# 58 expert blocks instead of 56 get their first product before the expert loop, and 0.62 and 2.0 gathers per block instead of 0.60 and 1.98

## The chip, the cores and the metric

The kernel runs on one core of a Trainium2 chip. The metric is the device time of one execution in microseconds. The core has a matrix engine (PE, with PEld for its weight loads), a vector engine (DVE), an activation engine (ACT), GpSimd (POOL), and SyncE (SP), which here only issues DMAs. Each engine works through its instructions in order. DMAs are issued on the queues of SP, POOL and ACT.

## The reference

Two groups of tokens (128 of a prompt, 512 of a latent grid, D = 1024) go through two layers that share their weights. Layer 0 mixes with a short gated convolution, layer 1 with a bidirectional Mamba-2 scan; each is followed by the channel mixer that this change touches, PEER:

```
q = (t @ wq).reshape(T, 8 heads, 2, 128);  s = einsum(q, keys)       # two lists of 128 scores
s1, i1 = top_k(s[:, :, 0], 16);  s2, i2 = top_k(s[:, :, 1], 16)
cand = s1[..., :, None] + s2[..., None, :]                            # 256 candidates
sc, pos = top_k(cand, 16);  idx = take(i1 * 128 + i2, pos);  g = softmax(sc)
act = einsum('td,thkd->thk', t, u[idx])                               # 16384 experts, rows of u and v
out = einsum('thk,thkd->td', gelu(act) * g, v[idx])
```

So every token picks 8 x 16 experts of 16384, and each expert is one row of `u` and one of `v`.

## The kernel before

**Two ways through the experts.** For 464 of the 512 latent tokens (ND) the kernel computes all experts densely. The 16384 experts are 128 blocks of 128. The first product of block a ("U block", `u_blocks`, L502) is a 128 x 464 matrix of u-rows times tokens: 8 slices of K, and `mm3` (L126) does each in three matmuls of split operands (hi*hi, hi*lo, lo*hi), so 24 matmuls of 464 columns. ACT takes the Gelu (L511) into a tile `ga` of the pool `ring`, which has LAG + 2 = 5 buffers. The second product ("V block", in the loop at L651) multiplies `ga` with the dense gate matrix of the block and accumulates v-rows: 24 matmuls as well, 18 into six PSUM banks `acc` and two times three into a rotating bank `rot`, which DVE adds into `sacc` (L647, L649). Gates are zero where a token did not pick an expert.

For the other 48 latent tokens and the 128 prompt tokens the kernel gathers the picked rows instead: NG = 16 + 32 + 128 = 176 gathers, each an indirect DMA on POOL's queue (L592) of 128 rows of u and v (1 MB) into one of three buffers `uv`; DVE makes the dot with the token rows `hrow` (L599) and adds gate times v-row to `cacc` (L609). The three groups of columns begin at gathers 0, 16 and 48 (G0). At 16 and 48 the token rows change: `next_rows` loads a new `hrow` over the old one, which has one buffer, and `last_tokens` folds `cacc` with small matmuls on PE (L622, L623).

**Order of the stages in one PEER layer.** Gates first (`peer_gates`, L751): queries, scores and top-k on DVE, then 29 chunks of one-hot products that write the dense gate matrix to `gdram` in device memory. Beside that DVE-heavy work PE has time, and `fill(ns)` (L521) lets it do U blocks in portions, eight steps to a block, each step counted as 650 ns; NSP caps how many blocks. A block below NSP has its `ga` stored to `adram` in device memory by POOL's queue (L513) and loaded again by SP's queue before its V block (`load_act`, L567).

Then the handover, in this order of the program (from L627): `gather(0)`, `gather(1)` and the first gate tile `gt` on POOL's queue, all U blocks up to NSP - 1 that are not done yet, `load_act` of blocks 0 to 2, `make_h(0)` and `make_h(1)` (gate times activation on DVE at L577, its rounding on ACT at L581, the rest on DVE at L586), and the last U block:

```
fill(0, NSP * KT - state["n"] - KT)
for a in range(LAG):
    load_act(a)
make_h(0); make_h(1)
fill(1e9)
```

**The loop** runs over a = 0 to 125. While a + LAG < NSP an iteration holds one V block and one `load_act`; after that one V block and U block a + LAG (L658). From the last chunks of the gates on the order of the instructions is that of the program (`manual_schedule`). Gathers are placed by a credit: each iteration adds GATHER[0] (no U block) or GATHER[1] (with one), and for each whole unit one gather, one dot and one addition are issued; an iteration ends its gathers early at a group's start. Loads of U, V and gate tiles run on SP's queue through `Stream` (L72): two raw buffers, ACT makes the high part (L92), DVE the low part (L101), and the load of the next block waits until the split two blocks before is done.

Of the kernel before, what the change touches and what calls it, by code (L numbers as in the profile page):

```python
# [31 lines left out]
HALF = 320  # L32
EPS = 1e-6
NBLK = 128
NSP = 56
LAG = 3
GA = 4
TB = 16
# [1 line left out]
SW = 64  # L40
CH = 5
FILL_Q = (0, 8500)
GATHER = (0.60, 1.98)
START = 4
MORE = (1, 1, 0, 4)
ADA_C = 16
# [70 lines left out]
class K:  # L117
# [28 lines left out]
    def run(s):  # L146
        nc, A = s.nc, s.A
        with ExitStack() as ctx:
# [4 lines left out]
            s.gdram = dram.tile([NBLK // GA, P, ND // SG, GA, SG], F32, name="gdram")  # L153
            s.adram = dram.tile([NSP, P, ND], F32, name="adram")
            s.sdram = dram.tile([1, 2, D], F32, name="sdram")
# [328 lines left out]
    def peer(s, i):  # L484
        nc, A = s.nc, s.A
        with ExitStack() as ctx:
# [15 lines left out]
            def u_blocks():  # L502
                for a in range(NBLK):
# [7 lines left out]
                    nc.scalar.activation(g, pa, AF.Gelu)  # L511
                    if a < NSP:
                        nc.gpsimd.dma_start(s.adram[a], g)  # L513
# [7 lines left out]
            def fill(ns, steps=0):  # L521

                state["owe"] += ns
                while (steps > 0 or ns and state["owe"] > 0) and state["n"] < NSP * KT:
                    t = next(ub)
                    if not steps:
                        state["owe"] -= t
                    steps -= 1 if steps else 0
                    state["n"] += 1
                U.split(state["n"] // KT + 2)  # L530
# [8 lines left out]
            with ExitStack() as mc:  # L539
# [27 lines left out]
                def load_act(a):  # L567
                    if a < NSP:
                        t = ring.tile([P, ND], F32, name="ga")
                        nc.sync.dma_start(t, s.adram[a])  # L570
                        ga[a] = t
# [60 lines left out]
                state["owe"] = 0  # L632
                fill(0, NSP * KT - state["n"] - KT)
                for a in range(LAG):
# [16 lines left out]
                for a in range(NBLK - 2):  # L651
                    V.high(a + 2)
                    if a + LAG >= NSP:
                        U.high(a + LAG + 2)
# [21 lines left out]

                    credit += GATHER[0] if a + LAG < NSP else GATHER[1]
                    due, before = 0, slot
# [793 lines left out]
```

## Time and profile before

| what | value |
|---|---|
| time, median of 3 runs | 4063.26 us (4061.71 to 4071.17) |
| profiled execution, its own time | 4057.71 us |
| its span, first to last instruction | 4056.0 us |
| granted PE clock, mean | 0.987 |
| busy: PE, DVE, ACT, POOL | 97%, 84%, 41%, 13% |
| DMA: moved, mean rate | 979.15 MB, 241 GB/s |

The two expert loops lie at about 787 to 1815 us and 2999 to 4027 us of the span. The profile's times are from the start of the span. An idle time is shown in square brackets behind an instruction, with what ended it. A busy PE is a pipeline of matmuls, each of which shows a duration longer than the distance to the next one.

### The profile page before, as it was taken

To read this page: it belongs to the slowest core of one execution; us is meant where nothing else is said; L and a number is where in the kernel's file an instruction comes from. 1 tells how busy PE (TensorE), PEld (TensorE's weight loads), DVE (VectorE), ACT (ScalarE), POOL (GpSimd) and SP (SyncE) were. 2 spreads that over 40 slices of the span, in tenths; PEclk is the share of its full clock that TensorE was granted. 3 is DMA by queue.
4 is the path that set the end of the run, shared out by engine and by line. 5 is a ranking of instruction groups with operands and counts; after the bars stand their busy time and mean duration, and the time that the engine had idled before them with its cause. 6 is when DMAs were issued, how large, how long until landed. Compare 5 with 4: busy or idle time off the path is not lost.

```text
span 4056.0 us, 59421 instructions
## 1 busy us (share of the span) xinstructions
PE 3915.4 (97%) x22237; PEld 3548.9 (87%) x22237; DVE 3394.0 (84%) x6512; ACT 1663.2 (41%) x3120; POOL 514.9 (13%) x695
## 2 busy tenths in 40 slices
PE   8999999899999999999999999999989999999998
PEld 6989988788888888888899998998878888888887
DVE  8978988588878888887999856998768888888887
ACT  5233344433334333336555644334433333343333
POOL 0010000011112212211110101000011111121211
PEclk9999999999999999999999999999999999999999
DMA  6643258988889989973333234226888898998995
GB/s 228 218 154 121 83 171 248 287 318 312 329 311 338 341 325 333 339 274 126 114 102 119 88 114 173 83 99 192 251 296 314 316 334 316 337 335 329 333 333 222
DMA packets 337451, 979.15 MB, mean 241 GB/s; under 512 B 39371, under 2 KB 174795, under 8 KB 291081
## 3 DMA queue, kind: packets, MB, share of 16 engines
q1 hardware_dynamic: 146922, 508.73, 35.7%
q0 software_dynamic: 64000, 398.47, 26.4%
q10 hardware_dynamic: 126240, 68.16, 5.9%
q8 instruction: 174, 2.85, 0.3%
q14 instruction: 115, 0.94, 0.1%
HBM read 867.00 MB, written 108.14 MB: 240 GB/s over the span
## 4 chain that ended last, share of the span: by engine, by line
issue 41%; PE 29%; DVE 15%; POOL 9%; DMA 4%; ACT 2%; POOLq 0%; SPq 0%; ACTq 0%; DVEq 0%
POOL uv L592 9%; PE pact L128 2%; DMA ur<-uT 2%; PE pact L130 2%; PE pj L128 2%; PE pact L129 2%; PE pj L129 2%; PE pj L130 2%; DVE ul L101 2%; DVE wl L101 1%; PE bank L128 1%; PE bank L129 1%; PE bank L130 1%; PE bank L1189 1%; PE pg L999 1%
## 5 line engine op out<-in xcount | busy, mean ns | idle before, releaser
L128 PE MATMUL pact<-hnh,uh 128*128 128x464 f32 x2048 | 774.2, 378 | 1.0 <-DVE xt L623 1.0
L130 PE MATMUL pact<-hnh,ul 128*128 128x464 f32 x2048 | 768.3, 375 | 0.0
L129 PE MATMUL pact<-hnl,uh 128*128 128x464 f32 x2048 | 766.6, 374 | 0.0
L592 POOL DMA_INDIRECT uv<-uv,cidx x352 | 362.2, 1029 | 1698.6 <-DVE cacc L609 1567.2
L128 PE MATMUL acc<-h,wh 128*128 128x464 f32 x1536 | 575.4, 375 | 0.0
L130 PE MATMUL acc<-h,wl 128*128 128x464 f32 x1536 | 575.3, 375 | 0.0
L129 PE MATMUL acc<-h,wh 128*128 128x464 f32 x1536 | 573.1, 373 | 0.0
L92 ACT ACTIVATE wh<-wr 128x1024 fp32r<-128x1024 f32 x385 | 404.9, 1052 | 377.8 <-DMA wr<-uv 92.5
L599 DVE SCALAR_TENSOR_TENSOR uv<-uv,hrow 128x1024 f32<-128x1024 f32 x352 | 430.1, 1222 | 128.5 <-DMA uv<-uv,cidx 125.3
L101 DVE TENSOR_TENSOR wl<-wr,wh 128x1024 fp32r<-128x1024 f32 x385 | 469.8, 1220 | 54.7 <-ACT wh L92 54.4
L609 DVE SCALAR_TENSOR_TENSOR cacc<-uv,dg,cacc 128x1024 f32<-128x1024 f32 x346 | 443.4, 1282 | 0.0
L130 PEld LDWEIGHTS pact<-hnh,ul 128*128 128x128 f32 x2048 | 386.4, 189 | 45.5 <-DVE ul L101 0.3
L128 PEld LDWEIGHTS pact<-hnh,uh 128*128 128x128 f32 x2048 | 387.2, 189 | 44.6 <-DVE xt L623 1.3
L129 PEld LDWEIGHTS pact<-hnl,uh 128*128 128x128 f32 x2048 | 387.2, 189 | 44.3
L511 ACT ACTIVATE ga<-pact 128x464 f32<-128x464 f32 x256 | 141.8, 554 | 582.6 <-PE pact L130 578.9
L101 DVE TENSOR_TENSOR ul<-ur,uh 128x1024 fp32r<-128x1024 f32 x256 | 312.1, 1220 | 56.0 <-ACT uh L92 55.9
L92 ACT ACTIVATE uh<-ur 128x1024 fp32r<-128x1024 f32 x256 | 268.3, 1050 | 184.7 <-PE pact L129 81.0
L129 PEld LDWEIGHTS acc<-h,wh 128*128 128x128 f32 x1536 | 291.0, 189 | 36.0
L130 PEld LDWEIGHTS acc<-h,wl 128*128 128x128 f32 x1536 | 290.0, 189 | 34.9
L128 PEld LDWEIGHTS acc<-h,wh 128*128 128x128 f32 x1536 | 290.7, 189 | 33.8
L601 ACT ACTIVATE dg<-dg 128x1 f32<-128x1 f32 x352 | 70.6, 200 | 540.4 <-DVE uv L599 540.0
L586 DVE TENSOR_TENSOR h<-h,h 128x464 fp32r<-128x464 f32 x256 | 163.8, 640 | 127.7 <-PE rot L129 123.8
(346 smaller groups left out, 7978.1 us busy)
## 6 DMA issues: line engine op xcount, KB each, us to landing
ur<-uT SPq DMA_DIRECT2D x256, 512.0 KB
wr<-uv SPq DMA_DIRECT2D x256, 512.0 KB
gt<-gdram SPq DMA_DIRECT2D x62, 928.0 KB
gdram<-st ACTq DMA_DIRECT2D x28, 2048.0 KB
mw<-ada_wT SPq DMA_DIRECT2D x80, 512.0 KB
adram<-ga POOLq DMA_DIRECT2D x112, 232.0 KB, 4.1
ga<-adram SPq DMA_DIRECT2D x112, 232.0 KB
wr<-ssd_w SPq DMA_DIRECT2D x48, 512.0 KB
```

The lines of the kernel that those rows point to most:

```text
L92: s.K.nc.scalar.activation(hi.rearrange("p a b -> p (a b)"), s.raw[s.nh], AF.Copy)
L101: s.K.nc.vector.tensor_sub(lo.rearrange("p a b -> p (a b)"), s.raw.pop(s.ns), hi.rearrange("p a b -> p (a b)").bitcast(F32))
L128: mm(out, wh, mh, start=start, stop=False)
L129: mm(out, wh, ml, start=False, stop=False)
L130: mm(out, wl, mh, start=False, stop=stop)
L511: nc.scalar.activation(g, pa, AF.Gelu)
L586: nc.vector.tensor_sub(h2, h, h1.bitcast(F32))
L592: nc.gpsimd.indirect_dma_start(out=t[:], out_offset=None, in_=A["uv"].rearrange("l e d -> (l e) d"), in_offset=bass.IndirectOffsetOnAxis(a ...
L599: nc.vector.scalar_tensor_tensor(UV[n][:, :D], UV[n][:, :D], 1.0, rows[-1], op0=ALU.mult, op1=ALU.mult, accum_out=dg[:, n:n + 1])
L601: nc.scalar.activation(dg[:, n:n + 1], dg[:, n:n + 1], AF.Gelu)
L609: nc.vector.scalar_tensor_tensor(cacc, t[:, D:], dg[:, n:n + 1], cacc, op0=ALU.mult, op1=ALU.add)
L999: nc.tensor.matmul(g[:, q, :], oh[:, t + q, :], o1[:, t + q, :], start=True, stop=False)
```

## The change

Two constants at the head of the file. NSP goes from 56 to 58: in each layer 58 blocks have their U product, their store to `adram` and their load from it ahead of the loop or in its first part, and `adram` has 58 slots. The loop has 55 iterations without a U block instead of 53, and 71 with one instead of 73 (two more at the end carry V alone in both). GATHER goes from (0.60, 1.98) to (0.62, 2.0).

```diff
-NSP = 56
+NSP = 58
 LAG = 3
@@
 FILL_Q = (0, 8500)
-GATHER = (0.60, 1.98)
+GATHER = (0.62, 2.0)
```

The places that read them: the cap of `fill` (L524), the store or keep decision (L512), `load_act` (L568), the handover (L633) and the loop (L653, L658, L677, L682).

## Rows read from the trace of the kernel before

**Rows 1.** The page, part 1: busy time, share of the span, instructions.

```profile
PE 3915.4 (97%) x22237; PEld 3548.9 (87%) x22237; DVE 3394.0 (84%) x6512; ACT 1663.2 (41%) x3120; POOL 514.9 (13%) x695
```

**Rows 2.** Waits of PE, whole span: who waited for whom, us, times, longest.

```profile
PE rot L128 <- ACT ga L511: 18.2, 2, 9.7
PE rot L128 <- DVE sacc L649: 15.8, 11, 3.9
...
PE rot L128 <- DVE sacc L647: 6.2, 2, 3.6
```

**Rows 3.** Timeline of PE, layer 0: start, us, engine, line, operation [idle before].

```profile
763.05 0.46 PE L128 MATMUL pact<-hnh,uh 128*128 128x464 f32 x1
...
778.05 0.38 PE L130 MATMUL pact<-hnh,ul 128*128 128x464 f32 x1
786.91 0.75 PE L128 MATMUL rot<-h,wh 128*128 128x464 f32 x1 [8.48 <-ACT ga L511]
...
796.54 0.67 PE L128 MATMUL rot<-h,wh 128*128 128x464 f32 x1 [3.61 <-DVE sacc L647]
```

**Rows 4.** Timeline of PE, the handover of layer 1.

```profile
2999.50 0.76 PE L128 MATMUL rot<-h,wh 128*128 128x464 f32 x1 [9.71 <-ACT ga L511]
```

**Rows 5.** Stretches: length, busy (count) of PE, PEld, DVE, ACT, POOL, PEclk, DMA share, GB/s.

```profile
849.00:899.00 50.00, 50.00 (x240) 44.68 (x239) 41.90 (x58) 18.34 (x33) 6.57 (x6) 1.00 0.90 326
1230.00:1330.00 100.00, 100.00 (x478) 89.26 (x477) 87.33 (x110) 39.10 (x80) 20.30 (x20) 1.00 0.91 346
```

**Rows 6.** Timeline of POOL, which issues its DMAs, at the handover.

```profile
774.45 0.59 POOL L564 DMA_DIRECT2D gt<-gdram  x1
775.01 1.66 POOL L513 DMA_DIRECT2D adram<-ga  x3
```

**Rows 7.** DMA queues from 773 to 785: packets, MB, share.

```profile
q0 software_dynamic: 599, 3.69, 87.4%
```

**Rows 8.** DMA queues from 785 to 787.

```profile
q0 software_dynamic: 25, 0.07, 8.8%
```

**Rows 9.** Timeline of DVE at the handover.

```profile
784.59 1.19 DVE L577 TENSOR_TENSOR h<-ga,gt 128x464 f32<-128x464 f32 x2 [8.41 <-DMA gt<-gdram]
```

**Rows 10.** DMA queues from 793 to 799: q1 is SP's, q0 POOL's.

```profile
q1 hardware_dynamic: 511, 1.36, 58.6%
q0 software_dynamic: 159, 1.07, 42.2%
```

**Rows 11.** Timeline of SP, which issues its DMAs, at the handover.

```profile
785.26 0.32 SPq L570 DMA_DIRECT2D ga<-adram  x1
785.68 0.42 SPq L84 DMA_DIRECT2D ur<-uT  x1
```

**Rows 12.** Waits of SP's queue from 763 to 800.

```profile
SPq L570 <- DVE h L577: 11.3, 1, 11.3
```

**Rows 13.** Timeline of ACT at the handover.

```profile
789.70 1.06 ACT L92 ACTIVATE uh<-ur 128x1024 fp32r<-128x1024 f32 x1 [2.84 <-DMA ur<-uT]
```

**Rows 14.** DMA issues of the whole span: count, KB each, median us to landing.

```profile
TT<-cdram POOLq DMA_DIRECT2D x40, 8.0 KB, 2.6
```

**Rows 15.** Stretches around gathers 16 and 48 in both layers, columns as above.

```profile
924.00:950.00 26.00, 25.35 (x120) 22.04 (x119) 17.30 (x26) 8.35 (x15) 3.12 (x3) 0.93 0.82 291
1142.00:1230.00 88.00, 84.69 (x400) 74.65 (x399) 67.49 (x86) 30.88 (x64) 17.19 (x16) 0.98 0.84 307
3131.00:3163.00 32.00, 29.84 (x143) 26.34 (x142) 21.65 (x32) 9.83 (x17) 3.13 (x3) 0.95 0.74 270
3365.00:3480.00 115.00, 112.67 (x540) 99.79 (x540) 95.31 (x122) 42.68 (x87) 22.19 (x22) 1.00 0.90 332
```

**Rows 16.** Timeline of SP at the change of `hrow` for gather 48.

```profile
1144.21 0.33 SPq L615 DMA_DIRECT2D hrow<-hdram  x1
```

**Rows 17.** Timeline of DVE at the same change.

```profile
1150.58 1.23 DVE L599 SCALAR_TENSOR_TENSOR uv<-uv,hrow 128x1024 f32<-128x1024 f32 x1 [1.05 <-DMA hrow<-hdram]
```

**Rows 18.** Timeline of PE at the folds there.

```profile
1156.69 1.87 PE L622 MATMUL pact<-fold,cacc 128*128 128x32 f32 x16
```

## The prediction

> **What bounds the kernel now.** I read the page first: PE is busy for 97% of the span [rows 1], so a change pays only where PE stands idle or runs for nothing. Next the list of who waited for whom, for PE over the whole span [rows 2]: the longest entry is two waits, one per layer, 18.2 us together, of `rot` for the Gelu at L511; two waits for the first copy into `sacc` (L647) add 6.2 us, and eleven for the sums at L649 15.8 us. Then the timeline of PE at the first two [rows 3, 4]. The reader is to see a handover. The last one-hot products end at 763.05, three U blocks follow back to back until 778.05 plus 0.21, then PE stands for 8.48 us, does seven eighths of V block 0, and stands for another 3.61 us. Layer 1 repeats it with 9.71 and 2.6 us. Last the stretches [rows 5]: in the loops PE is busy for all of 50 and all of 100 us, 478 matmuls in 100 us or 0.209 us each, 24 of them or 5.02 us per block, with the DMA engines busy for 90 and 91%. So the loops are paced by PE with DMA close behind, and the handover is where PE has nothing to do.
>
> **What the change moves.** The fills beside the gates ask for about 416 steps of U work (8 by number, 265.6 us at 0.65 us), that is 52 blocks; 53 were done at 763.05. The old cap of 56 is not reached there, so nothing beside the gates changes. The two added blocks run in the handover, behind the three that run there today: 48 matmuls at 0.209 are 10.0 us of PE in each layer. The same 10.0 us leave the loop: two iterations fewer carry a U block. PE's total is unchanged, and the gain is as much of 10.0 us per layer as falls into time in which PE is idle.
>
> **What ends the gap, step by step (layer 0).** POOL's queue issues two gathers (1.05 MB each), the gate tile `gt` at 774.45 (0.95 MB) and from 775.01 the stores of the last three U results (0.24 MB each) [rows 6]; that makes 3.76 MB. POOL's queue moved 3.69 MB of it between 773 and 785 [rows 7] and the last 0.07 MB after [rows 8], so the burst ends at about 785.3. The product at L577 waits 8.41 us for `gt` until 784.59 [rows 9], and 2.32 us later (two products, two roundings, the Gelu of block 55 behind them on ACT) PE starts at 786.91 [rows 3].
>
> With 58, PE has blocks 53 to 56 and 57 to do: 778.3 + 10.0 = 788.3, if their U data is there. It is: the loads have a buffer as soon as the split two blocks before is done, so the two added ones go out by about 771 and 776, ahead of the three `adram` loads on SP's queue. Two costs come with them.
>
> First, the load at 776 moves 0.52 MB beside the burst. [rows 10] show a stretch where both queues have work, and both move: 1.36 and 1.07 MB in 6 us. At the burst's 0.31 MB per us the burst then ends 1.7 us later, at 787.0; the bounds are 0 (the load is served after it) and 3.4 (both added loads fall into it). The Trainium skill (DMA: Bandwidth & Descriptors, section Queues, rings and completion order) says that each DMA engine takes turns between the queues that have work, a packet at a time. By that rule the 1.7 us are due; if queues were served in order of issue, the term would be 0 and each layer would gain 1.7 us more.
>
> Second, the ring of activations has five buffers. Today `adram` loads 0 and 1 find two that are free long before, and only load 2 is late: it goes out at 785.26 [rows 11], having waited 11.3 us for the first product at L577 to end [rows 12]. With 58 the five buffers hold blocks 52 to 56, so loads 0, 1 and 2 all wait for stores that stand at the end of POOL's burst. Load 0 goes out at 787.0 instead of before 770, and the first product waits for it, no longer for `gt`. Its landing: a U load of 512 KB took 4.0 us (785.68 to 789.70 [rows 11, 13]) and an 8 KB load 2.6 us [rows 14]; for 232 KB I take 3.2, so 790.2, and with the same 2.32 us PE starts at 792.5. The idle time falls from 8.5 to 4.2 us.
>
> The second stall is set by ACT, which in order waits 2.84 us for the next U load until 789.70 [rows 13]; 6.84 us after that PE goes on at 796.54. That load now stands behind three loads instead of one: about 788.3 to issue, 4.0 to land, 0.3 for the data ahead of it, so 792.6, and PE goes on at 799.4. (PE by itself gets there at 792.5 + 6.02 = 798.5, the 6.02 being 796.54 - 3.61 - 786.91.) So PE goes on 2.9 us later than today with 10.0 us more behind it: **7.1 us per layer, 14 for both**; layer 1 runs the same chain against a gap of 9.7 us [rows 4]. Bounds: 20 us if all of the added work is covered, 9 if burst and landing take their upper values (795.0 and 801.8: 4.7 per layer).
>
> **The gathers.** From the code's own arithmetic, 31 gathers in the 53 U-free iterations become 34 in 55, and the rest go from 145 in 73 (with one iteration of three and two of one) to 142 in 71, all of two. DMA per U-free iteration: V 0.52, activation 0.24, gate 0.24, gathers 0.62 x 1.05 = 0.65, in all 1.65 MB in 5.02 us or 328 GB/s; with two gathers and a U load 3.38 MB in 10.04 us, 337. The trace carries 346 for 100 us with PE busy throughout [rows 5], so both fit, by a few per cent. The extra stores and loads of activations (two of each per layer, 0.95 MB) are in these sums.
>
> The change of `hrow` at gather 48 becomes dearer in one way and cheaper in another. Today it costs PE, counted as stretch less 0.209 per large matmul (all but the 16 folds): 88 - 384 x 0.209 = 7.7 us and 115 - 524 x 0.209 = 5.5 us [rows 15], part of it from the iteration of three gathers after it. With 58 gathers 46 and 47 fall into one iteration, so the load of the new rows, which took 6.4 us from issue to the dot that uses it (1144.21 to 1150.58 [rows 16, 17]), stands between them: dot 47 at 1149.5 (today's 1150.58 less its wait of 1.05), the load issued behind it at 1150.7 and landed at 1157.1, its dot and addition 47 behind it until about 1159.5 (2.4, the 1.22 of L599 and 1.28 of L609 overlapping), against folds that start at 1156.69 today [rows 18]: 2.8 us of PE. Add 1.9 for the folds [rows 18] and 1.8 for the lower granted clock (1.2 of 2.4 GHz) behind such a stop (0.07 of 26 us around gather 16 [rows 15]): 6.5, or 13.0 for both layers against 13.2. I take 0 (-8 to +6). The change at gather 16 costs 26 - 104 x 0.209 = 4.3 and 32 - 127 x 0.209 = 5.5 us today [rows 15]; it moves one iteration forward, away from the iteration that loads a gate tile: -1 (-4 to +3).
>
> **Sum.** -14 + 0 - 1 = -15 us against the profiled execution's 4057.7 (span 4056.0): 4042.7. That execution lies 5.6 us under the median of the three timed runs, 4063.3, so the median becomes **4048**.
>
> **Rivals.**
> 1. *The gap is covered altogether* (-20 and cheap `hrow` changes, -5: 4038). For it: 8.5 + 3.6 and 9.7 + 2.6 us of idle time exceed 10.0. Against it: the ring wait, which puts a load between the burst and the first product.
> 2. *The gap only moves* (about -6: 4057). Loads 0 to 2 and the U load after them wait behind a burst that the added stores and loads lengthen by more than I took; the lower bound above, 9, less what dearer `hrow` changes cost, some 3. For it: DMA is at 0.31 MB per us there and everything in the chain is a transfer.
> 3. *Slower*: the loop with two gathers in each of 71 iterations does not catch up after the `hrow` stall at gather 48. There PE waits for L649 each time that DVE is late; DMA demand (337) is within 3% of the 346 that it carried, and today's iterations of one gather give relief that is gone. At 0.2 us lost in each of the some 64 iterations behind it, in both layers, it costs 26: -15 + 26 = +11, 4074. It decides from 0.12 us per iteration. Against it: today some ten iterations of two gathers in a row keep PE busy for all of 100 us [rows 5].
> 4. *Not what it says*: the added blocks would have to run beside the gates and delay them; the fills' budget, under the old cap already, speaks against it. It is no case of its own.
>
> **Numbers.** What a measurement of this kernel can tell from no change is about 0.3%, 12.2 us. Forecast (12 to 20 us faster) 0.56; rival 1 0.08; rival 2, widened to everything within 12 us, 0.29; rival 3 0.07. So faster 0.64, same 0.29, slower 0.07. The range reaches from rival 1 to just under no change: 4036 to 4062.
>
> **What would show it.** After the last one-hot product: five U blocks in a row, then a gap of 4 us (3 to 7) ended by the Gelu at L511, with L577 waiting for `ga<-adram` and not for `gt`, and all three `adram` loads on SP's queue issued after the burst. The second gap under 2 us. U-free iterations at 5.02 us, others at 10.1. In the iteration with gathers 46 and 47 the dot (L599) waits some 4.5 us for `hrow`. I am wrong if L577 still waits for `gt`, if U loads starve the two added blocks, or if the waits for L649 grow along the loop.

## The result, and the profile after

The changed kernel takes 4043.83 us in the median of four runs (4038.93 to 4046.46), the kernel before 4062.49 (4057.68 to 4071.17) beside it. The ratio is 0.9945 with an interval of 0.9927 to 0.9963: 0.55% or 18.7 us faster. A later comparison gave 4038.71 and 0.9949 (0.9937 to 0.9961). The forecast of 4048 us was 4 to 9 us too slow.

The profiled execution of the changed kernel, 4046.46 us (span 4044.7, mean granted clock 0.986), is the slowest of its four, and that of before, 4057.71, nearly the fastest of its own. By the two traces the difference is therefore only 11.3 us. I cut both into stages. From the first U block behind the last one-hot products to the end of the expert loop, layer 0 takes 1051.5 us before and 1037.9 after, layer 1 1052.4 and 1047.8: 18.1 us less. All that lies outside, which the change doesn't touch, came out 6.8 us longer in this execution. Some of it comes ahead of layer 0's handover and shifts its times: 765.32 - 763.05 = 2.3 us.

The page's busy times [rows 1] hardly move, as the prediction said of PE's total:

```profile
PE 3916.6 (97%) x22237; PEld 3550.5 (88%) x22237; DVE 3396.1 (84%) x6512; ACT 1664.8 (41%) x3120; POOL 518.5 (13%) x699
```

The list of who waited for whom, for PE over the whole span, answers to [rows 2] (us in all, times, longest):

```profile
PE rot L128 <- ACT ga L511: 8.9, 2, 4.9
PE rot L128 <- DVE sacc L649: 8.6, 7, 4.0
...
PE rot L128 <- DVE sacc L647: 3.3, 2, 1.7
```

18.2 became 8.9, 6.2 became 3.3, 15.8 became 8.6. Here is PE's timeline after, the handover of layer 0 and then of layer 1, against [rows 3, 4]:

```profile
765.32 0.46 PE L128 MATMUL pact<-hnh,uh 128*128 128x464 f32 x1
...
790.39 0.38 PE L130 MATMUL pact<-hnh,ul 128*128 128x464 f32 x1
794.78 0.48 PE L128 MATMUL rot<-h,wh 128*128 128x464 f32 x1 [4.01 <-ACT ga L511]
...
802.66 0.48 PE L128 MATMUL rot<-h,wh 128*128 128x464 f32 x1 [1.63 <-DVE sacc L647]
...
2996.32 0.76 PE L128 MATMUL rot<-h,wh 128*128 128x464 f32 x1 [4.94 <-ACT ga L511]
...
3004.68 0.48 PE L128 MATMUL rot<-h,wh 128*128 128x464 f32 x1 [1.68 <-DVE sacc L647]
```

Five U blocks run back to back from 765.32 to 790.6, then come gaps of 4.01 and 1.63 us where 8.48 and 3.61 stood, and in layer 1 4.94 and 1.68 for 9.71 and 2.6. POOL's timeline shows the burst, and below it SP's the loads behind it:

```profile
776.94 0.61 POOL L564 DMA_DIRECT2D gt<-gdram  x1
777.50 1.68 POOL L513 DMA_DIRECT2D adram<-ga  x3
781.58 0.55 POOL L513 DMA_DIRECT2D adram<-ga  x1 [2.40 <-ACT ga L511]
786.62 0.54 POOL L513 DMA_DIRECT2D adram<-ga  x1 [4.49 <-ACT ga L511]
```

```profile
789.50 1.40 SPq L570 DMA_DIRECT2D ga<-adram  x3
791.00 0.37 SPq L84 DMA_DIRECT2D ur<-uT  x1
```

The same handover in the waits of SP's queue, and on DVE:

```profile
SPq L570 <- DMA adram<-ga: 10.8, 3, 10.4
```

```profile
792.46 1.19 DVE L577 TENSOR_TENSOR h<-ga,gt 128x464 f32<-128x464 f32 x2 [1.41 <-DMA ga<-adram]
```

All three loads go out together at 789.50, after stores instead of after DVE as in [rows 12], and L577 waits for `ga<-adram`, not for `gt` [rows 9].

The stretches answer to [rows 5] and [rows 15] (columns as there: length, busy time and count of PE, PEld, DVE, ACT, POOL, granted clock, DMA share, GB/s):

```profile
1230.00:1330.00 100.00, 100.00 (x477) 89.32 (x476) 84.58 (x107) 38.57 (x80) 20.33 (x20) 1.00 0.90 332
923.00:949.00 26.00, 26.00 (x133) 23.42 (x132) 20.13 (x31) 9.44 (x16) 3.34 (x3) 1.00 0.89 333
3125.00:3157.00 32.00, 32.00 (x161) 28.75 (x161) 26.13 (x38) 11.47 (x20) 4.30 (x4) 1.00 0.87 322
1138.00:1226.00 88.00, 86.06 (x410) 76.55 (x409) 73.38 (x94) 33.82 (x69) 17.05 (x17) 0.98 0.90 330
3343.00:3458.00 115.00, 110.15 (x517) 98.24 (x517) 92.09 (x116) 40.79 (x85) 20.37 (x21) 0.97 0.90 317
```

The loop still keeps PE busy for all of 100 us. Around gather 16 (second and third line) PE doesn't stop any more. Around gather 48 layer 0 lost less than before and layer 1 more.

For the experiments I took from each trace the time of every iteration and subtracted 5.044 us for one without and 10.09 us for one with a U block; what is left is called lost. The handover runs from the first U block after the one-hot products to the start of the `acc` products of V block 1. In the last row, 1.9 us of each entry are matmuls of the last two V blocks and no loss.

| us, layer 0 / layer 1 | before | after | after, again | e1 | e2 | e4 | e5 | e6 (60) |
|---|---|---|---|---|---|---|---|---|
| handover | 35.9 / 36.3 | 38.7 / 40.1 | 40.2 / 40.0 | 39.4 / 40.5 | 36.4 / 37.1 | 39.8 / 40.9 | 38.9 / 40.4 | 44.6 / 44.7 |
| less 10.08 per two added blocks | 35.9 / 36.3 | 28.6 / 30.0 | 30.1 / 29.9 | 29.3 / 30.4 | 36.4 / 37.1 | 29.7 / 30.9 | 28.8 / 30.4 | 24.4 / 24.5 |
| lost around gather 16 | 4.6 / 5.8 | 1.8 / 1.8 | 2.2 / 1.8 | 3.6 / 6.4 | 2.5 / 1.8 | 4.2 / 2.7 | 3.6 / 5.7 | 3.1 / 3.5 |
| lost around gather 48 | 7.6 / 5.1 | 5.7 / 10.0 | 3.0 / 8.1 | 7.2 / 11.7 | 5.4 / 9.4 | 2.5 / 4.0 | 3.8 / 9.7 | 6.7 / 4.2 |
| lost in iterations 122 to 125 | 3.5 / 3.8 | 5.1 / 3.5 | 4.8 / 3.7 | 16.2 / 16.0 | 2.9 / 2.9 | 4.6 / 3.5 | 3.6 / 5.1 | 3.5 / 3.5 |

### The profile page after: what moved, and what is told of

Its sections match the earlier page's. It is cut to its first block, busy times and chain, and to the rows that moved or that the text cites. A ratio compares the mean times of both kernels' runs of the same rounds, so it can differ in the third digit from the quotient of the medians.

```text
span 4044.7 us, 59437 instructions
## 1 busy us (share of the span) xinstructions
PE 3916.6 (97%) x22237; PEld 3550.5 (88%) x22237; DVE 3396.1 (84%) x6512; ACT 1664.8 (41%) x3120; POOL 518.5 (13%) x699
## 3 DMA queue, kind: packets, MB, share of 16 engines
q1 hardware_dynamic: 147498, 509.68, 36.3%
q8 instruction: 174, 2.85, 0.3%
## 4 chain that ended last, share of the span: by engine, by line
issue 41%; PE 29%; DVE 15%; POOL 9%; DMA 4%; ACT 2%; POOLq 0%; SPq 0%; ACTq 0%; DVEq 0%
POOL uv L592 9%; DMA ur<-uT 2%; PE pact L128 2%; PE pact L130 2%; PE pact L129 2%; PE pj L128 2%; PE pj L129 2%; PE pj L130 2%; DVE ul L101 2%; DVE wl L101 1%; PE bank L128 1%; PE bank L129 1%; PE bank L130 1%; PE bank L1189 1%; PE pg L999 1%
```

## The experiments

The theory to test was that of the prediction with one term enlarged: about 13.5 us from the handover, where transfers set the end, and some 7 from the rates, because the change of `hrow` at gather 16 leaves the iteration that also loads a gate tile.

Each diff below is against the changed kernel.

**The two constants one by one.** e1 has NSP alone, e2 the rates alone:

```diff
-GATHER = (0.62, 2.0)
+GATHER = (0.60, 1.98)
```

> 58 blocks with the old gather rates (0.60, 1.98). Theory (two gains: the handover, 13.5 us in the two traces together, and the cheaper change of `hrow` at gather 16, 6.7 us, which the new rates bring by moving it from iteration 26 to 25, away from the load of a gate tile): the handover gain stays, the change at gather 16 costs 4 to 6 us per layer as in the kernel before, and five gathers are left for the last iteration, some 5 us per layer for the three more; about 13.5 - 10 = 3 us faster than before, 4059 (4050 to 4066). Rival (the gain is the handover alone and the rates only keep the count right): apart from the last iteration all of it is there, and the stretch around gather 16 costs 1.8 us per layer as after the change.

```diff
-NSP = 58
+NSP = 56
```

> 56 blocks with the new gather rates (0.62, 2.0). Theory: no gain in the handover (gaps of 8.5 and 3.6, 9.7 and 2.6 us as before), the change of `hrow` at gather 16 falls to 1.8 us per layer (-7 in both), the change at gather 48 is exposed as after the change (6 to 10 us per layer, +3 in both): about 4 us faster than before, 4058 (4052 to 4064). Rival (the stretch around gather 16 was cheaper by chance of that execution): it costs 4 to 6 us per layer here and the time is that of before, 4062.

e1 took 4071.97 us, a ratio of 1.0029 (1.0014 to 1.0043): slower. e2 took 4050.74, 0.9974 (0.9964 to 0.9984). In the table e1 has the handover of the changed kernel and the gather 16 of before, and e2 the reverse, so each constant does its own part. e2 gained 9.5 us (4060.25 to 4050.74), more than twice the 4 expected: its trace loses 6.1 us less at gather 16, as the theory says, and 5.0 less in iterations 119 to 121, which it doesn't explain. But e1 loses 12.5 us more per layer at the end, where I had expected some 5. By the old rates 58 blocks leave too many gathers, and the last iteration, 125, has to finish the last five (it counts by the second rate, but has no U block: those end in iteration 124). Three of them are still to be issued there, and four dots to be made. POOL's timeline in e1 at the end of layer 0, these three, and then PE's:

```profile
1796.76 1.09 POOL L592 DMA_INDIRECT uv<-uv,cidx  x1 [3.80 <-DVE cacc L609]
1802.16 0.94 POOL L592 DMA_INDIRECT uv<-uv,cidx  x1 [4.32 <-DVE cacc L609]
1805.13 0.94 POOL L592 DMA_INDIRECT uv<-uv,cidx  x1 [2.03 <-DVE cacc L609]
```

```profile
1814.01 0.75 PE L128 MATMUL rot<-h,wh 128*128 128x464 f32 x1 [9.98 <-ACT wh L92]
```

ACT rounds `wh` for the next V block only behind the gate factors of these four dots, so PE stands for 9.98 us. The rates are thus worth about 10 us by themselves and some 30 where NSP is 58.

**The ring of activations.** In e3 the last six U results are stored on ACT's queue, so that loads 0 to 2 need not wait for the end of POOL's burst.

```diff
-                        nc.gpsimd.dma_start(s.adram[a], g)
+                        (nc.scalar if a >= NSP - 6 else nc.gpsimd).dma_start(s.adram[a], g)
```

> The changed kernel, but the last six U results are stored to `adram` from ACT's queue instead of POOL's, so their stores no longer stand behind two gathers and the gate tile, and their ring buffers come free early. Theory (the first gap of the handover is the ring: loads 0 to 2 wait for stores at the end of POOL's burst, and the U load behind them sets the second gap): loads 0 to 2 go out some 5 us earlier, the product at L577 waits for `gt` again, the first gap falls from 4.0 and 4.9 to about 1 us, the second to under 0.5; 5 us per layer, 10 in all: 4034. Rival (the handover is bound by the bytes of the burst): the loads fall into the burst and delay `gt` by what they gain; the gaps stay within 1 us of what they are and the time stays at 4044.

It took 4037.97 us, 0.9945 (0.9932 to 0.9959), like the changed kernel. The first two loads did go out earlier, the first of them 19.2 us behind the first U block (767.05 here) instead of 24.2 (789.50 - 765.32), yet nothing was won: the handover takes 40.9 and 40.6 us. SP's timeline and its waits (765 to 806), POOL's third gather, then ACT's and PE's timelines in e3, layer 0:

```profile
785.55 0.33 SPq L84 DMA_DIRECT2D ur<-uT  x1
786.23 5.49 SPq L570 DMA_DIRECT2D ga<-adram  x3
```

```profile
SPq L570 <- DMA adram<-ga: 10.6, 2, 7.1
```

```profile
779.92 0.97 POOL L592 DMA_INDIRECT uv<-uv,cidx  x1 [0.30 <-issue]
```

```profile
773.89 1.06 ACT L92 ACTIVATE uh<-ur 128x1024 fp32r<-128x1024 f32 x1 [5.56 <-issue]
...
794.90 1.06 ACT L92 ACTIVATE uh<-ur 128x1024 fp32r<-128x1024 f32 x1 [2.07 <-DMA ur<-uT]
```

```profile
774.99 0.71 PE L128 MATMUL pact<-hnh,uh 128*128 128x464 f32 x1 [2.65 <-ACT uh L92]
...
799.45 0.48 PE L128 MATMUL rot<-h,wh 128*128 128x464 f32 x1 [2.17 <-ACT ga L511]
```

ACT was held up for 5.56 us by its own store, which cost PE 2.65 us, and the U load of 785.55 landed only for 794.90. The ring's wait was shortened for two loads, but not removed: the loads still waited 10.6 us in all for stores, against 10.8 after the change, and the third went out at 791.40. And POOL's queue, rid of the stores, sent the third gather at 779.92, which goes out at 795.87 in the changed kernel, so the same stretch had 1 MB more to move. So e3 shows that this edit wins nothing; what the handover would be without the ring's wait stays open.

**The place of the first gathers in the queue.** e9 (58) and e9b (56, old rates: the same edit of the kernel before) issue `gather(0)` and `gather(1)` behind the gate tile and the stores.

```diff
-                gather(0)
-                gather(1)
                 load_g(0)
...
                 fill(0, NSP * KT - state["n"] - KT)
+                gather(0)
+                gather(1)
```

> The changed kernel with the first two gathers issued behind the gate tile and behind the stores of the U blocks before the last, instead of ahead of them all; nothing else moves. Theory (the handover waits for the gate tile and for stores that stand behind 2.1 MB of gathers on POOL's queue): the gate tile lands some 6 us earlier, load 0 goes out before PE has done its blocks, the first gap falls below 1 us and the second below 1; some 5 us per layer, 4034. Rival (the bytes decide, not their order): the gathers then run against the next gate tile and the U and V loads, the second gap grows by what the first loses, and the time stays at 4044.

> The kernel before the change, 56 blocks and the old rates, with the same reordering. Theory (the added blocks pay only by covering the wait for the gate tile): with the tile 6 us earlier, the first gap falls from 8.5 and 9.7 to 2 to 4 us and the second closes; 8 to 10 us per layer without any added block, 4044 against 4062, so that in this order the added blocks are worth only what is left of the gap, 2 to 4 us per layer. Rival (the gap is set elsewhere: by the ring or by the bytes): less than 4 us per layer, 4055 or more.

e9 took 4035.55 us, 0.9946 (0.9927 to 0.9965); e9b 4063.37, 1.0012 (1.0000 to 1.0023). PE in e9, both layers, then PE and ACT in e9b, layer 0:

```profile
795.14 0.48 PE L128 MATMUL rot<-h,wh 128*128 128x464 f32 x1 [0.70 <-ACT ga L511]
805.75 0.76 PE L128 MATMUL rot<-h,wh 128*128 128x464 f32 x1 [5.92 <-DVE sacc L647]
...
2993.73 0.48 PE L128 MATMUL rot<-h,wh 128*128 128x464 f32 x1 [0.70 <-ACT ga L511]
3002.53 0.76 PE L128 MATMUL rot<-h,wh 128*128 128x464 f32 x1 [4.10 <-DVE sacc L647]
```

```profile
784.05 0.48 PE L128 MATMUL rot<-h,wh 128*128 128x464 f32 x1 [2.54 <-ACT ga L511]
801.29 0.76 PE L128 MATMUL rot<-h,wh 128*128 128x464 f32 x1 [12.54 <-DVE sacc L647]
```

```profile
794.46 1.06 ACT L92 ACTIVATE uh<-ur 128x1024 fp32r<-128x1024 f32 x1 [10.46 <-DMA ur<-uT]
```

In layer 0 the first gap shrinks and the second grows by more: 4.01 + 1.63 became 0.70 + 5.92, and 8.48 + 3.61 became 2.54 + 12.54. In layer 1 e9 comes out 1.8 us shorter (4.94 + 1.68 became 0.70 + 4.10) and e9b 2.1 longer (9.71 + 2.63 became 4.29 + 10.13). My theory, that the order on POOL's queue costs the time, fell: neither kernel is faster for it. The rival, that the bytes of the handover do, is what these gaps and times look like, but they don't prove it: in e9 a part of the second gap is the first dot, which stands ahead of further products in DVE's order and now waits for its gather, 2.85 and 2.03 us.

**More work to cover it.** e6 has 60 blocks and e11 62, with rates that spread the gathers again.

```diff
-NSP = 58
+NSP = 60
-GATHER = (0.62, 2.0)
+GATHER = (0.67, 2.0)
```

> The changed kernel with 60 blocks and 0.67 gathers per iteration without a U block (38 in 57, two in each of 69). Theory (a block pays as far as it falls into idle time of the handover): the first gap, 4.0 and 4.9 us after the change, closes; PE goes on 5 to 7 us later with 10.0 us more done, so 3 to 5 us per layer, 4036; the gathers ask for 1.70 MB in 5.02 us, 338 GB/s, near the 346 carried, and may give back some. Rival (each added block lengthens POOL's burst by its own load and the ring wait moves with it, so the gaps stay): nothing gained, 4044 or slower.

```diff
-NSP = 58
+NSP = 62
-GATHER = (0.62, 2.0)
+GATHER = (0.705, 2.0)
-                slot, credit = 0, 0.0
+                slot, credit = 0, 0.6
```

> The changed kernel with 62 blocks, 0.705 and a credit that starts at 0.6 (40 gathers in 59 iterations, two in each of 67). Theory (a block pays as far as it falls into idle time of the handover, and with 60 blocks the two gaps and the slow start behind them were down to some 3.6 us per layer): at most 3.6 us per layer beyond 60 blocks, less what the denser gathers cost (1.71 MB in 5.02 us, 341 GB/s against 346 carried): 4032 (4026 to 4042). Rival (each two blocks bring 5 us per layer, as from 58 to 60): 4024.

e6 took 4034.18 us, 0.9940 (0.9918 to 0.9961); e11 4034.56, 0.9947 (0.9932 to 0.9963). (By the code e11 has 42 gathers in its 59 iterations, not the 40 of the expectation.) PE in e6, layer 0:

```profile
804.38 0.48 PE L128 MATMUL rot<-h,wh 128*128 128x464 f32 x1 [0.70 <-ACT ga L511]
811.04 0.48 PE L128 MATMUL rot<-h,wh 128*128 128x464 f32 x1 [1.97 <-DVE sacc L647]
```

Layer 1 has 0.69 and 1.97, e11 0.70 and 1.98 in both layers, and its handover, less 10.08 per two added blocks, takes 24.1 and 24.2 us like that of e6. So at 60 the transfers are covered: what is left is the way from PE over ACT and DVE and back, and further blocks have nothing to fill. In the traces the handover of e6 is 4.2 us (layer 0) and 5.5 us (layer 1) shorter than that of the changed kernel (table, second row); in time e6 is not to be told from 58.

**Moving the gathers out of the handover.** e14 puts gathers 0 and 1 into iteration 1 of the program and the first dot into iteration 3.

```diff
-GATHER = (0.62, 2.0)
+GATHER = (0.665, 2.0)
-                gather(0)
-                gather(1)
...
-                dot(0)
-                slot, credit = 0, 0.0
+                slot, credit = 0, -2.0
...
+                    if a == 1:
+                        gather(0)
+                        gather(1)
+                    if a == 3:
+                        dot(0)
```

> The changed kernel with the first two gathers issued in iteration 1 of the loop and the first dot in iteration 3, outside the handover; 0.665 for 0.62 and a credit that starts at -2, so that the same 34 gathers fit into the iterations without a U block. Theory (the order on POOL's queue only moved idle time from the first gap to the second; what sets the two together is the bytes that must move before the second product can run): with 2.1 MB less, some 6 us at 0.31 to 0.35 MB per us, the handover becomes bound by PE: both gaps under 1.5 us, 5 to 7 us per layer faster; the loop gives back some at 0.665 and at gather 16, now in iteration 27: 4034 (4030 to 4040). Rival (a wait in the chain, the ring's loads or ACT's order, not the bytes): both gaps together stay at 5 us or more, 4043 or slower.

It took 4049.39 us, 0.9971 (0.9958 to 0.9984), some 11 us more than the changed kernel beside it. Its twelve executions spread from 4033.68 to 4060.15, and the trace is of one of 4040.94. PE, POOL and ACT in layer 0:

```profile
789.53 0.48 PE L128 MATMUL rot<-h,wh 128*128 128x464 f32 x1 [0.69 <-ACT ga L511]
796.07 0.48 PE L128 MATMUL rot<-h,wh 128*128 128x464 f32 x1 [1.84 <-DVE sacc L644]
808.48 0.76 PE L128 MATMUL rot<-h,wh 128*128 128x464 f32 x1 [5.55 <-DVE sacc L644]
```

```profile
790.62 1.02 POOL L592 DMA_INDIRECT uv<-uv,cidx  x1 [0.31 <-issue]
791.95 0.97 POOL L592 DMA_INDIRECT uv<-uv,cidx  x1 [0.30 <-issue]
793.23 1.36 POOL L592 DMA_INDIRECT uv<-uv,cidx  x1 [0.30 <-issue]
```

```profile
805.56 1.06 ACT L92 ACTIVATE wh<-wr 128x1024 fp32r<-128x1024 f32 x1 [11.16 <-DMA wr<-uv]
```

The first gap closes; the second stays at 1.84 us in layer 0 and falls to 0.30 in layer 1. The handover is 4.2 and 7.6 us shorter than after the change, but in layer 0 the same transfers then stop iteration 1, and iterations 1 and 2 lose 9.5 us. The gathers were put off less than the text of the program says: POOL's queue has nothing ahead of them to wait for but the last store, so three go out at 790.62 to 793.23, right behind it, before the V loads that SP issues from 793.43. In layer 1 (gaps of 0.69, 0.30 and 1.46) iterations 1 and 2 lose 1.7 us only, so there the theory's gain did come. There the gathers went out more slowly and V loads in between; whether that is the reason was not tried. The rest of the loss is at gather 16, 7.1 and 4.1 us more than after the change (below).

**Where gathers 14 to 16 fall.** e5 shifts the changed kernel's gathers so that 14, 15 and 16 fall into the iterations of before.

```diff
-                slot, credit = 0, 0.0
+                slot, credit = 0, -GATHER[0]
...
-                    credit += GATHER[0] if a + LAG < NSP else GATHER[1]
+                    credit += (GATHER[0] if a + LAG < NSP else GATHER[1]) + (GATHER[0] if a == 40 else 0)
```

> The changed kernel with every gather up to iteration 39 one iteration later (the credit starts 0.62 lower and gets it back in iteration 40), so that gather 15 and the change of `hrow` fall into iteration 26 again, which also loads a gate tile; the rest of the schedule is that of the change. Theory (the stretch around gather 16 costs 1.8 us per layer when the `hrow` load goes out an iteration and more from the gate tile's, and 4 to 6 when it goes out just ahead of it): the stretch from iteration 23 to 31 costs 4 to 6 us per layer, 2 to 4 more than after the change; 5 us in all, 4049. Rival (the new rates themselves are cheaper there, by their spacing): 1.8 us per layer and the time of the changed kernel, 4044.

e4 and e10 drop the credit left over when a group begins, which parts gathers 46 and 47; e10 was meant to keep gather 15 in iteration 25 as well.

```diff
-GATHER = (0.62, 2.0)
+GATHER = (0.64, 2.0)
...
+                    if due and slot + due in G0:
+                        credit %= 1
```

> The changed kernel with 0.64 for 0.62 and the credit left over at a group's start dropped: 35 gathers in the iterations without a U block, gather 47 alone in iteration 61, two in each other iteration with a U block. Theory (after the change the load of `hrow` between gathers 46 and 47 of one iteration is exposed, 5.7 and 9.9 us around gather 48 in the two layers): with a whole iteration between them the dot no longer waits for `hrow`, and the stretch costs about 3 us per layer (the folds and the lower clock behind them): 2 to 7 us faster per layer, 4035 (4030 to 4041). Rival (the cost is that of the folds and the clock, whichever gathers stand beside them): it stays at 5 to 10 us per layer and the time at 4044.

```diff
-GATHER = (0.62, 2.0)
+GATHER = (0.645, 2.0)
...
-                slot, credit = 0, 0.0
+                slot, credit = 0, -0.2
...
+                    if due and slot + due in G0:
+                        credit %= 1
```

> The changed kernel with 0.645, a credit that starts at -0.2 and the credit left over at a group's start dropped: gather 47 alone in iteration 61, and gather 15 in iteration 25 as after the change. Theory (both changes of `hrow` in the place where they cost least): the stretch around gather 16 costs 1.8 us per layer and that around gather 48 2.5 to 4 against 3.4 to 9.9; 2 to 4 us per layer faster than the changed kernel: 4037. Rival (these costs are given back elsewhere): the time of the changed kernel.

e5: 4046.01 us, 0.9970 (0.9959 to 0.9981). e4: 4035.76, 0.9949 (0.9936 to 0.9963). e10: 4048.91, 0.9975 (0.9963 to 0.9986), 12 us over what I had expected. The code's own arithmetic gives the iterations, the traces what they lose:

| kernels | gathers 14, 15, 16 in iterations | lost there, us, layer 0 / layer 1 |
|---|---|---|
| after, after again, e2, e3, e9 | 24, 25, 27 | 1.8 / 1.8, 2.2 / 1.8, 2.5 / 1.8, 1.8 / 1.8, 1.8 / 1.8 |
| before, e1, e5, e9b | 25, 26, 28 | 4.6 / 5.8, 3.6 / 6.4, 3.6 / 5.7, 6.1 / 6.0 |
| e4 | 23, 24, 26 | 4.2 / 2.7 |
| e6 | 22, 23, 25 | 3.1 / 3.5 |
| e11 | 20, 21, 23 | 3.5 / 2.8 |
| e10 | 23, 25, 26 | 8.2 / 8.1 |
| e14 | 25, 27, 28 | 8.9 / 5.9 |

A gate tile is loaded in iterations 22, 26, 30. In the pattern of before it goes out just ahead of the first activation and V loads that the next products need. In e5, layer 1, DVE waits for one and PE stops two iterations after the fold:

```profile
3143.26 0.64 DVE L577 TENSOR_TENSOR h<-ga,gt 128x464 f32<-128x464 f32 x1 [3.14 <-DMA ga<-adram]
```

```profile
3148.68 0.48 PE L128 MATMUL rot<-h,wh 128*128 128x464 f32 x1 [2.06 <-DVE sacc L649]
```

The changed kernel has neither line in that stretch. So the term comes from the iterations into which the gathers fall, and e5, which keeps the new rates, gives it back: 1.8 + 3.9 us. That the gate tile's load is what makes these iterations dear is read from this order and this wait; e4, e6 and e11 lose 2.7 to 4.2 us with the gathers in others, so it is not the only cost. The two worst rows have gathers 15 and 16 in neighbouring iterations. ACT in e10, layer 0, shows what is late there, a V load:

```profile
928.51 1.06 ACT L92 ACTIVATE wh<-wr 128x1024 fp32r<-128x1024 f32 x1 [6.96 <-DMA wr<-uv]
```

e10's miss is this: 6.4 and 6.3 us more than the changed kernel, together about the 12 us missing. In e4 the gathers are parted, and it loses 2.5 and 4.0 us around gather 48, like e10. That is 3.2 and 5.9 us less than in the first trace of the changed kernel and 0.5 and 4.1 less than in the second; but e3 and e9, which have the gathers of the changed kernel, lose only 4.0 and 3.7, and 3.4 and 4.8. So a saving by parting them is not shown. At gather 16 e4 loses 2.4 and 0.9 us more; in the time nothing of it is to be seen.

**The changed kernel again**, unaltered, beside e10, e11 and e14:

> The changed kernel, unaltered, beside the three others: 0.993 to 0.996 of the kernel before, 4043. In its trace the handover is as in the first profile (gaps of 4 to 5 and 1.6 us), the stretch around gather 16 costs 1.8 us per layer; the stretch around gather 48 varies between 3.4 and 10 us.

4038.71 us, 0.9949 (0.9937 to 0.9961), with the handover and the gather 16 of its first trace (table).

## Why the prediction was right, and which term was mis-sized

- *What moves.* Right: the blocks beside the gates are the same, five U blocks in a row follow.
- *The burst.* Forecast: 1.7 us later, at 787.0, loads behind it. With the shift of 2.3 that is 789.3; the loads went out at 789.50 and were there for 792.46, after 3.0 us where 3.2 had been taken. The DMA queues between 776 and 787 show both at work:

```profile
q0 software_dynamic: 405, 2.94, 76.9%
q1 hardware_dynamic: 192, 0.67, 17.3%
```

  POOL's queue moved 2.94 MB in 11 us, 0.27 MB per us against 0.31 [rows 7], while SP's had 0.67. The Trainium skill (DMA: Bandwidth & Descriptors, section Queues, rings and completion order) says that each DMA engine takes turns between the queues that have work. The trace agrees with it: both queues moved data in the same 11 us.
- *First gap.* Forecast PE at 792.5, so 794.8 with the shift, and a gap of 4.2 us; measured 794.78 and 4.01. Layer 1: 4.94.
- *Second gap.* Forecast 799.4, so 801.7, and under 2 us; measured 802.66 and 1.63. The U load was 0.9 us later than forecast, and PE went on 6.84 us behind its rounding on ACT, as before:

```profile
795.82 1.06 ACT L92 ACTIVATE uh<-ur 128x1024 fp32r<-128x1024 f32 x1 [1.09 <-DMA ur<-uT]
```

  The handover gained 7.3 and 6.3 us net of the 10.08 that moved, against 7.1 each.
- *The ring.* The wait came as described, on the right tile. How much it costs is not shown: e3 was to take it away, but only shortened it for two of three loads and moved a gather into the same stretch.
- *Gather 48.* Forecast 0 (-8 to +6), with a dot that waits 4.5 us for `hrow`. DVE after, layers 0 and 1, against [rows 17]:

```profile
1148.48 1.23 DVE L599 SCALAR_TENSOR_TENSOR uv<-uv,hrow 128x1024 f32<-128x1024 f32 x1 [1.55 <-DMA hrow<-hdram]
...
3352.98 1.23 DVE L599 SCALAR_TENSOR_TENSOR uv<-uv,hrow 128x1024 f32<-128x1024 f32 x1 [4.46 <-DMA hrow<-hdram]
```

  4.46 us came in layer 1; in layer 0 the rows needed 3.3 us from their issue at 1145.21 instead of 6.4, and the wait was 1.55. Around gather 48 that makes -1.9 and +4.9 against before in the first trace, -4.7 and +3.0 in the second: +3 and -2 for both layers, about nothing. That it came out so near to 0 is in part luck: with the same gathers the two layers together lose 7.7 us in e3 and 15.7 in the first trace.
- *Gather 16: the term that was mis-sized.* I named the move away from the gate tile's iteration, which e5 bears out, and took -1 us for both layers, with -4 as the end. Measured: 10.4 before, 3.6 after, -6.8. I had counted the loss of before and then assumed that most of it belongs to the fold and stays; the fold itself costs 1.8 us. This is most of the 4 to 9 us by which the forecast was too slow.
- *Rival 1* (all covered) takes 60 blocks. *Rival 2* (the gap only moves) is what reordering does in three of four handovers (e9, e9b), not what added work does. *Rival 3* (the loop falls behind) did not come: waits for L649 fell from 15.8 to 8.6 us.

Open: iterations 119 to 121, where `x` is loaded, lose 1.6 to 8.4 us from kernel to kernel, and nothing that I changed explains it. In its two traces the changed kernel loses 2.4 and 5.6 us less there than before, for both layers together; that much of the gain has no cause shown.

## What to carry to other kernels

Where transfers set the end of a handover, moving them in their queue can just move the gap, as it did here in three of four handovers, while independent work of the waiting engine filled it; add such work until the gap stops shrinking, here at 60 blocks, and expect the last part to be too small to time. When work leaves a loop, whatever is rationed by iteration must be rationed anew: the same NSP was 0.3% slower or 0.55% faster by the rates beside it. A rate also decides which iterations coincide; list from the code which loads fall into the iteration of a rare event before a cost is put on the rate.

## What was not expected of the hardware

- A 0.52 MB load took 4.0 us in the handover of before [rows 11, 13]. The one that e14's layer 0 issued at 793.43, right behind three gathers, was there only for 805.56: 12.1 us.
- An instruction's place in the program doesn't hold a queue back: three gathers written into the loop's iteration 1 or later went out at 790.62 to 793.23, while PE had barely begun V block 0.
- A store issued on ACT's queue stopped ACT's own arithmetic for 5.56 us in e3's layer 0 and 5.08 in layer 1. It was the first of six in each layer, right behind the store of the last gates on the same queue; the other five took 0.33 or 0.34 us to issue.
